# Attention of a hybrid decoder step: each head runs its four pairs of query blocks in a row, operands in pieces

## The chip, the cores and the metric

The kernel runs on one core of a Trainium2 chip. The metric is the device time of one execution in microseconds. The core has five engines, each with its own instruction queue: TensorE (PE; PEld are its weight loads), VectorE (DVE), ScalarE (ACT), GpSimd (POOL) and SyncE (SP), which issues the DMA transfers here. An engine works through its queue in order; between engines, semaphores make an instruction wait for its operands.

## What is computed

One layer of a hybrid decoder for a prompt of 1024 rows and 32 decode rows (8 sequences of 4). RMSNorm and one input projection feed a gated linear recurrence (4 heads) and a forgetting attention (8 heads of 64); both are gated, concatenated, projected back, added to x and normed. The change lies in the attention of the prompt, here for blocks of 128 queries (qb, cb: rows of q and c of the block; scale = D ** -0.5):

```python
def fox_prompt(q, k, v, log_f):
    c = jnp.cumsum(log_f, axis=1).transpose(0, 2, 1)
    ...
    def block(i):
        ...
        s = jnp.einsum('bqhd,bkhd->bhqk', qb, k).astype(jnp.float32) * scale
        s = s + (cb[..., None] - c[:, :, None, :])
        s = jnp.where(qpos[:, None] >= kpos[None, :], s, -jnp.inf)
        p = jax.nn.softmax(s, axis=-1)
        return jnp.einsum('bhqk,bkhd->bqhd', p.astype(v.dtype), v)
    o = lax.map(block, jnp.arange(nb))
    ...
```

## The kernel before

All matmuls keep fp32 accuracy by splitting operands into a high part (rounded to the fast fp32r format) and a low part (the rest), so a product of two operands takes three matmuls.

The order of all engines' work is written by hand (`manual_schedule`), by a Python program that mixes two strands. The first is the main loop: log-forget sums, the recurrence for four heads, then 32 attention steps. The second is the *stream*, a generator (`projections`) that yields a few matmuls at a time with an estimate of their time: the slabs of the input projection (128 columns each; `slab` L441 to 460, three chunks of 352 rows and 24 matmuls each, 0.45 us estimated for three), the values' transposes (`fox_values`), the gates (`fox_gate`), and later the output projection and the decode attention. `fill(us)` lets the stream go on for so many estimated microseconds. When the stream stands at a flag that the main loop has not raised (`wait_flag`), it yields nothing and the rest of that fill is lost. `need(mark)` runs the stream up to a mark. `defer(n, f)` records f after n more stream yields.

The attention works on four pairs of heads; a pair's q, k and v come from three slabs (buffers u0, u2, u5), its gate from a fourth. A *step* (`fox_step`) is one head and 256 queries, with q = 0 to 3 for the place of these queries in the prompt. It transposes the softmax rows of its two blocks (T, tile pt, L925), copies and subtracts them into a high and a low part (ACT L929, DVE L930), weighs the values with them (W, tile po), and meanwhile makes the scores (S, tile ps, three banks) of the next step's second block and the second-next step's first block: mask sum L894, reduction L895, exponential L905 with its row sum, reciprocal L908 on DVE, scaling L910 on POOL. `PLANS` gives the order within a step, with fractions at which the step's fill is spent. Work and widths grow with q.

Before the scores of a head can be made, `fox_prep` forms its operands: Q1 and K1 hold the high part of q or k in 64 partitions and the log-forget sums in the others (two small DMA loads from c_s), Q2 and K2 the high and low parts: two copies on ACT (L846, L852), two on DVE (L848, L851), one subtraction on POOL (L854) and one on DVE (L856), each over whole rows of 1024. The heads of a pair have separate buffers. The steps of a pair run in the order (head, q) = (0,0), (0,1), (1,0), (1,1), (0,2), (0,3), (1,2), (1,3), and both heads' preparation for the next pair stands in its last steps.

## Time and profile before

| | us |
|---|---|
| median of 3 timed runs | 782.65 (782.34 to 782.94) |
| profiled execution, its time | 779.85 |
| its span, first to last instruction | 778.1 |
| PE busy | 740.7 (95%) |
| DVE busy | 461.8 (59%) |
| ACT busy | 356.9 (46%) |
| POOL busy | 319.4 (41%) |

The span falls into the start and value projection (0 to some 90 us), gates and recurrence under which the slabs are made (to 350), the attention of the first three pairs under the remaining slabs (to 600), the last pair under output projection and decode attention (to 712), and the rest of the output projection. An engine's busy time in a stretch, set against the length of the stretch, tells how much of it the engine stood still; what ended a wait is given in brackets behind an instruction.

### The profile page before, as it was taken

Reading aid. Unit: us, or ns where it says so; the run is one execution under the profiler, and the core shown is the slowest. Engines: PE = TensorE matmul, PEld = TensorE weight load, DVE = VectorE, ACT = ScalarE, POOL = GpSimd, SP = SyncE. Lnnn points to the kernel's source line nnn. Section 1 sums busy time; section 2 is a strip of 40 time slices with the busy share of each in tenths; the row PEclk is TensorE's granted clock in tenths of the full one; section 3 lists DMA queues with packets and bytes.
Section 4 is the critical chain, followed back from the end, with each engine's and each line's share of the span. In section 5 each row is a group of like instructions: output and inputs, shape, how many; then the busy total and the mean of one; then the engine's idle time right before and its main releaser. Section 6 shows DMA issues by size and latency. Waiting matters only on the chain.

```text
span 778.1 us, 12930 instructions
## 1 busy us (share of the span) xinstructions
PE 740.7 (95%) x4815; PEld 659.7 (85%) x4815; DVE 461.8 (59%) x954; ACT 356.9 (46%) x833; POOL 319.4 (41%) x337
## 2 busy tenths in 40 slices
PE   6999899999999999998999989989999899999996
PEld 5678899998999999997998889979988676577886
DVE  7774324646647665267447844785478776667422
ACT  4562446444242441136546654757466522455312
POOL 4450435373471853535434462536344533332101
PEclk8999999999999999999999999999999999999999
DMA  8411000100221103003101020101111686713521
GB/s 300 134 34 34 1 29 3 60 26 36 84 80 59 55 31 109 29 32 123 44 28 57 29 82 28 57 29 55 55 56 57 210 304 221 258 56 130 190 81 55
DMA packets 28465, 64.99 MB, mean 84 GB/s; under 512 B 6290, under 2 KB 7442, under 8 KB 28402
## 3 DMA queue, kind: packets, MB, share of 16 engines
q1 hardware_dynamic: 28402, 64.16, 23.6%
q8 instruction: 38, 0.62, 0.3%
q14 instruction: 25, 0.20, 0.1%
HBM read 47.27 MB, written 16.88 MB: 82 GB/s over the span
## 4 chain that ended last, share of the span: by engine, by line
PE 71%; DVE 15%; ACT 7%; issue 4%; POOL 1%; DMA 1%; SPq 0%; DVEq 0%; ACTq 0%; POOLq 0%
PE pj L95 52%; PE ps L95 11%; PE po L95 3%; DVE u L856 2%; PE pt L925 2%; DVE u L930 2%; DVE st L895 2%; PE pt L95 1%; ACT u L905 1%; ACT u L929 1%; DMA u<-in_w_dram 1%; DVE u L812 1%; ACT xhi L269 1%; POOL u L311 1%; DVE u L791 1%
## 5 line engine op out<-in xcount | busy, mean ns | idle before, releaser
L95 PE MATMUL pj<-xhi,u 128*128 128x352 f32 x1152 | 315.2, 332 | 0.7 <-DVE u L449 0.5
L95 PEld LDWEIGHTS pj<-xhi,u 128*128 128x128 f32 x1152 | 205.8, 188 | 3.4 <-DVE u L449 0.8
L95 PE MATMUL pj<-xlo,u 128*128 128x352 f32 x576 | 186.2, 323 | 0.0
L95 PE MATMUL ps<-u,u 128*128 128x64 f32 (+7 forms) x952 | 129.7, 272 | 3.4 <-ACT u L905 2.6
L95 PEld LDWEIGHTS ps<-u,u 128*128 128x128 f32 (+2 forms) x952 | 111.8, 178 | 14.4 <-ACT u L905 4.4
L910 POOL TENSOR_SCALAR u<-u,st 128x128 f32<-128x128 f32 (+3 forms) x64 | 48.7, 761 | 153.8 <-DVE st L908 87.7
L95 PEld LDWEIGHTS pj<-xlo,u 128*128 128x128 f32 x576 | 108.6, 189 | 0.7
L95 PE MATMUL pj<-u,xhi 128*128 128x260 f32 (+1 forms) x384 | 90.3, 329 | 4.1 <-DVE u L488 2.2
L905 ACT ACTIVATE u<-ps,st 128x512 f32<-128x512 f32 (+2 forms) x96 | 55.0, 578 | 50.3 <-DVE st L898 21.6
L95 PE MATMUL pj<-h,u 128*128 128x512 f32 (+2 forms) x237 | 74.3, 384 | 0.8 <-DVE h L1046 0.8
L655 POOL TENSOR_TENSOR u<-u,u 128x256 f32<-128x256 f32 (+1 forms) x56 | 40.4, 721 | 84.4 <-PE ps L95 78.8
L95 PEld LDWEIGHTS pj<-u,xhi 128*128 128x128 f32 x384 | 63.9, 191 | 12.2 <-ACT xhi L269 2.5
L930 DVE TENSOR_TENSOR u<-pt,u 128x512 fp32r<-128x512 f32 (+1 forms) x80 | 48.5, 631 | 29.3 <-ACT u L929 28.7
L95 PE MATMUL pj<-u,xlo 128*128 128x260 f32 (+1 forms) x192 | 62.6, 326 | 2.9 <-DVE xlo L273 2.9
L95 PE MATMUL po<-u,u 128*128 128x256 f32 (+1 forms) x320 | 52.3, 287 | 9.3 <-DVE u L930 4.7
L929 ACT ACTIVATE u<-pt 128x512 fp32r<-128x512 f32 (+1 forms) x80 | 41.8, 552 | 41.9 <-PE pt L925 34.2
L895 DVE TENSOR_REDUCE st<-ps 128x1 f32<-128x512 f32 (+2 forms) x96 | 53.3, 556 | 12.4 <-PE ps L95 9.8
L95 PEld LDWEIGHTS po<-u,u 128*128 128x128 f32 x320 | 44.3, 188 | 16.7 <-DVE u L930 7.8
L95 PEld LDWEIGHTS pj<-h,u 128*128 128x128 f32 (+1 forms) x237 | 42.3, 185 | 10.7 <-ACT u L811 1.2
L95 PE MATMUL pj<-u,u 128*128 128x512 f32 (+3 forms) x174 | 46.8, 437 | 2.7 <-ACT u L1213 2.1
L95 PE MATMUL pj<-w,u 128*128 128x512 f32 (+2 forms) x125 | 47.8, 383 | 0.0
L656 POOL TENSOR_TENSOR u<-u,u 128x256 f32<-128x256 f32 (+1 forms) x56 | 43.7, 780 | 0.0
(242 smaller groups left out, 1144.0 us busy)
## 6 DMA issues: line engine op xcount, KB each, us to landing
u<-in_w_s_dram SPq DMA_DIRECT2D x24, 512.0 KB
out_dram<-u SPq DMA_DIRECT2D x12, 512.0 KB
u<-in_x_b_dram SPq DMA_DIRECT2D x8, 512.0 KB
u<-in_cache_k_t_dram SPq DMA_DIRECT2D x16, 256.0 KB
u<-in_cache_v_dram SPq DMA_DIRECT2D x16, 256.0 KB
m_s<-u SPq DMA_DIRECT2D x7, 512.0 KB
u<-m_s SPq DMA_DIRECT2D x14, 256.0 KB
w<-in_w_out_dram SPq DMA_DIRECT2D x12, 256.0 KB
```

The source lines that it names most:

```text
L95: PE.matmul(out, lhsT, rhs, start=start, stop=stop, skip_group_check=True)
L269: A.activation(xhi[:, k, t0:t0 + n], xt[:, k], AF.Copy)
L311: se[a].tensor_sub(l[:, a], raw[:, a], f32(h[:, a]))
L655: G.tensor_mul(k4[:, :, 0, :], k4[:, :, 0, :], f3[:, eb, 1:2].to_broadcast([128, n, m]))
L656: G.tensor_mul(q4[:, :, 1, :], q4[:, :, 1, :], f3[:, eb, 0:1].to_broadcast([128, n, m]))
L856: V.tensor_sub(K2[o], kf[r, :T], f32(K1[r]))
L895: V.tensor_reduce(st[:, m:m + 1], ps, axis=AX.X, op=OP.min)
L905: A.activation(P[:, s], ps, AF.Exp, scale=-1.0, bias=st[:, lo:lo + 1], accum_out=st[:, 2 + m:3 + m])
L910: G.tensor_scalar(P[:, :e], P[:, :e], st[:, 4:5], 1.0, op0=OP.mult, op1=OP.mult)
L925: PE.transpose(p[:, c:c + 128], probs[n, b][:, j * 128:(j + 1) * 128], ident)
L929: A.activation(ph[:, :w], p[:, :w], AF.Copy)
L930: V.tensor_sub(pl[:, :w], p[:, :w], f32(ph[:, :w]))
```

## The change

Four things change. The order of the steps: each head now runs q = 0, 1, 2, 3 in a row. The fills: a table per pair and step in place of four numbers by q and a factor for the last pair. The operands: they are made in pieces of a chunk (352 or 320 columns) or half a row (512); for head 0 of the later pairs the pieces are deferred from the eviction of each chunk of the q and k slabs, for head 1 they run as eight pieces over the last step of a pair and the first steps of the next; the query's subtraction is on DVE, not on POOL. The stream's wait ahead of the next pair's slabs: it was the flag that both heads are prepared, now a flag `free` raised after the second step of the pair, since head 1's preparation still reads u0 and u2 until then.

```diff
         i = slabs.index(C_FQ + pr * 128)
         qf, kf, vf = U(0), U(2), U(5)
-        yield from slab(i, f"fq{pr}", lambda ps, a, b: A.activation(qf[:, a:b], ps, AF.Copy, scale=-FD ** -0.5))
+
+        def evac(dst, which, scale):
+            def f(ps, a, b):
+                A.activation(dst[:, a:b], ps, AF.Copy, scale=scale)
+                if pr:
+                    defer(2, operand_hi, pr, 0, which, slice(a, min(b, T)))
+                    defer(5, operand_lo, pr, 0, which, slice(a, min(b, T)))
+            return f
+
+        if pr:
+            sums_in(pr, 0)
+        yield from slab(i, f"fq{pr}", evac(qf, 0, -FD ** -0.5))
         V.tensor_copy(qd[:, pr], qf[:, T:])
-        yield from slab(i + 1, f"fk{pr}", lambda ps, a, b: A.activation(kf[:, a:b], ps, AF.Copy))
+        yield from slab(i + 1, f"fk{pr}", evac(kf, 1, 1.0))
...
+    def operand_hi(pr, i, which, t):
+        r, o = slice(64 * i, 64 * i + 64), slice(64 - 64 * i, 128 - 64 * i)
+        x, X1, X2 = U((0, 2)[which]), QS(i)[which], QS(i)[2 + which]
+        V.tensor_copy(X1[r, t], x[r, t])
+        A.activation(X2[r if which else o, t], x[r, t], AF.Copy)
+
+    def operand_lo(pr, i, which, t):
...
+        V.tensor_sub(X2[o if which else r, t], x[r, t], f32(X1[r, t]))
+        if which and t.stop == T:
+            flags.add(f"prep{pr}{i}")
+
     def fox_prep(pr, i):
 
-        h, qf, kf = 2 * pr + i, U(0), U(2)
...
-        A.activation(Q2[o], qf[r, :T], AF.Copy)
-        SP.dma_start(f32(Q1[b0:b0 + 2]), cr)
-        V.tensor_copy(Q1[r], qf[r, :T])
-        SP.dma_start(f32(K1[b0 + 2:b0 + 4]), cr)
-        V.tensor_copy(K1[r], kf[r, :T])
-        A.activation(K2[r], kf[r, :T], AF.Copy)
-        G.tensor_sub(Q2[r], qf[r, :T], f32(Q1[r]))
-        V.tensor_sub(K2[o], kf[r, :T], f32(K1[r]))
+        sums_in(pr, i)
+        for c in range(2):
+            for which in range(2):
+                operand_hi(pr, i, which, slice(512 * c, 512 * c + 512))
+                yield
+                operand_lo(pr, i, which, slice(512 * c, 512 * c + 512))
+                yield
...
-    order = [(pr, i, q) for pr in range(4) for i, q in ((0, 0), (0, 1), (1, 0), (1, 1), (0, 2), (0, 3), (1, 2), (1, 3))]
+    order = [(pr, i, q) for pr in range(4) for i in range(2) for q in range(4)]
...
-        po, tt = po_[0], tt2[:, i]
+        po, tt = po_[0], tt2[:, n // 2 % 2]
...
-                yield from wait_flag(f"prep{pr}1")
+                yield from wait_flag(f"free{pr}")
...
     for i in range(2):
-        preps.append(fox_prep(0, i))
+        fox_const(i)
+    preps.append(fox_prep(0, 0))
+    for _ in range(8):
         fill(0.6)
-        fox_const(i)
-        for _ in range(4):
-            prep_step()
-            fill(0.77)
+        prep_step()
+    preps.append(fox_prep(0, 1))
...
+    FILL = ((4.8, 6.8, 6.2, 5.4) * 2,) * 3 + ((4.8, 6.8, 8.5, 8.0, 11.0, 10.5, 8.5, 7.0),)
     for n, (pr, i, q) in enumerate(order):
         s = n % 8
+        fox_step(n, FILL[pr][s])
         if pr == 3 and s == 0:
+            prep_step(True)
             flags.add("values")
             for k in range(4):
                 m_load(k, 0)
             for k in range(2):
-                defer(8 + 4 * k, m_split, k, 0)
-        fox_step(n, (7.6, 6.4, 4.4, 3.0)[q] * (F3 if pr == 3 else 1))
-        prep_step(True)
-        if s == 4 and pr < 3:
+                defer(7 + 3 * k, m_split, k, 0)
+        if s == 1:
+            prep_step(True)
+            flags.add(f"free{pr}")
+        if s == 6 and pr < 3:
             need(f"fk{pr + 1}")
-            preps.append(fox_prep(pr + 1, 0))
-        if s == 6 and pr < 3:
             preps.append(fox_prep(pr + 1, 1))
+        if s == 7 and pr < 3:
             need(f"v{pr + 1}")
```

In the changed program most lines stand further down: the copies of operands are L861 and L862, their subtraction L867, the values' eviction, cast and subtraction L796, L802 and L803, the mask sum, reduction and exponential L915, L916 and L926, the turned rows' copy and subtraction L950 and L951.

PE in pair 0, second step: the end of its weighing (po) and the scores (ps) that follow. Before, with the stream's slab (pj) around them:

```order
L95 MATMUL po_105<-u_3375,u_3252 128x128
L95 MATMUL pj_184<-xhi,u_732 128x352
L95 MATMUL pj_184<-xlo,u_732 128x352
L95 MATMUL pj_184<-xhi,u_733 128x352
...
L95 MATMUL ps_147<-u_3273,u_3272 128x384
L95 MATMUL ps_147<-u_3284,u_3283 128x384
L95 MATMUL pj_183<-xhi,u_732 128x352
```

Now, up to the third step's scores:

```order
L95 MATMUL po_105<-u_3350,u_3256 128x128
L95 MATMUL ps_146<-u_3234,u_3233 128x512
...
L95 MATMUL ps_147<-u_3242,u_3241 128x384
L946 MATMUL pt_1143<-cc,u_95 128x128
...
L946 MATMUL pt_1144<-cc,u_96 128x128
L95 MATMUL ps_145<-u_3234,u_3233 128x512
...
L95 MATMUL ps_146<-u_3242,u_3241 128x512
L95 MATMUL pj_183<-xhi,u_732 128x352
```

Before, 18 matmuls of the stream stand between weighing and scores and 18 behind them; now weighing, scores, the third step's transposes (pt) and its scores follow each other with none between.

DVE in the last steps of pair 0. Before, around the key's subtraction L856 (st are the row statistics):

```order
L895 TENSOR_REDUCE st_1105<-ps_147 128x1
L898 TENSOR_REDUCE st_1105<-st_1105 128x1
L856 TENSOR_TENSOR u_3238<-u_1118,u_3234 64x1024
L957 TENSOR_TENSOR u_101<-u_101,po_105 64x512
L907 TENSOR_REDUCE st_1105<-st_1105 128x1
L908 RECIPROCAL st_1105<-st_1105 128x1
L930 TENSOR_TENSOR u_3375<-pt_1143,u_3374 128x512
```

Now, in the last step, with pieces for head 1 of the next pair:

```order
L916 TENSOR_REDUCE st_1102<-ps_145 128x1
L861 CAST u_3237<-u_1117 64x512
L867 TENSOR_TENSOR u_3383<-u_1117,u_3237 64x512
L951 TENSOR_TENSOR u_3350<-pt_1144,u_3349 128x512
L951 TENSOR_TENSOR u_3350<-pt_1143,u_3349 128x384
L929 RECIPROCAL st_1102<-st_1102 128x1
L861 CAST u_3238<-u_1118 64x512
L915 TENSOR_TENSOR ps_146<-ps_146,cc 128x128
L916 TENSOR_REDUCE st_1103<-ps_146 128x1
L867 TENSOR_TENSOR u_3384<-u_1118,u_3238 64x512
L802 CAST u_4055<-u_100 128x4x64
```

The one subtraction over 1024 columns has become pieces of 512 between the steps' own instructions, and the values' casts follow them.

ACT at the first values (u_100 takes them from the transposes pt). Before:

```order
L774 ACTIVATE u_1115<-pj_183 128x352
L846 ACTIVATE u_3237<-u_1117 64x1024
L852 ACTIVATE u_3238<-u_1118 64x1024
L785 ACTIVATE u_100<-pt_1143 128x512
L785 ACTIVATE u_100<-pt_1144 128x512
```

Now:

```order
L785 ACTIVATE u_1115<-pj_183 128x352
L862 ACTIVATE u_3241<-u_1117 64x512
L862 ACTIVATE u_3242<-u_1118 64x512
L796 ACTIVATE u_100<-pt_1143 128x512
L862 ACTIVATE u_3241<-u_1117 64x512
L796 ACTIVATE u_100<-pt_1144 128x512
```

Two half rows instead of two whole rows stand ahead of the first of the values' evictions.

## Rows read from the trace of the kernel before

**Rows 1.** The page: span, and each engine's busy time, share, instructions.

```profile
span 778.1 us, 12930 instructions
PE 740.7 (95%) x4815; PEld 659.7 (85%) x4815; DVE 461.8 (59%) x954; ACT 356.9 (46%) x833; POOL 319.4 (41%) x337
```

**Rows 2.** By stretch: length; busy time (instructions) by engine; granted clock, DMA share, GB/s.

```profile
340.00:376.00 36.00, 33.04 (x206) 31.14 (x205) 26.42 (x51) 21.10 (x49) 16.33 (x16) 1.00 0.25 90
376.00:420.00 44.00, 43.99 (x293) 42.93 (x292) 20.90 (x57) 23.20 (x55) 17.38 (x17) 1.00 0.14 48
420.00:452.00 32.00, 26.99 (x175) 24.22 (x174) 27.62 (x52) 20.08 (x48) 17.40 (x15) 1.00 0.10 36
452.00:496.00 44.00, 44.00 (x292) 43.26 (x290) 19.80 (x56) 23.36 (x61) 18.00 (x20) 1.00 0.10 38
496.00:532.00 36.00, 31.65 (x208) 28.77 (x207) 30.99 (x61) 24.30 (x53) 17.19 (x16) 1.00 0.13 47
576.00:600.00 24.00, 21.25 (x144) 19.16 (x143) 20.91 (x46) 16.62 (x36) 10.06 (x10) 1.00 0.20 68
612.00:624.00 12.00, 8.56 (x29) 5.68 (x29) 7.16 (x11) 3.76 (x8) 5.29 (x6) 0.86 0.84 300
```

**Rows 3.** Order of time, first values: start, length, engine, line [idle before, releaser].

```profile
354.11 1.05 ACT L846 ACTIVATE u<-u 64x1024 fp32r<-64x1024 f32 x1
355.18 1.06 ACT L852 ACTIVATE u<-u 64x1024 fp32r<-64x1024 f32 x1
356.76 0.28 PE L795 MATMUL pt<-cc,u 128*32 128x128 f32 x1 [2.08 <-ACT u L785]
356.81 0.41 PE L95 MATMUL pj<-xhi,u 128*128 128x352 f32 x1
...
360.77 0.34 PE L95 MATMUL ps<-u,u 128*128 128x128 f32 x2
```

**Rows 4.** Order of time, from the first mask sum to the first weighing.

```profile
362.10 0.30 DVE L894 TENSOR_TENSOR ps<-ps,cc 128x128 f32<-128x128 f32 x1
...
365.68 0.82 POOL L910 TENSOR_SCALAR u<-u,st 128x128 f32<-128x128 f32 x2
...
368.91 0.48 ACT L929 ACTIVATE u<-pt 128x384 fp32r<-128x384 f32 x1
...
370.03 0.56 PE L95 MATMUL po<-u,u 128*128 128x256 f32 x3 [0.20 <-DVE u L930]
```

**Rows 5.** One line's instructions: count, ns min/median/max, first and last start.

```profile
L856 DVE TENSOR_TENSOR u<-u,u x8: 1221/3084/3391, 351.8 to 601.1; 64x1024 fp32r<-64x1024 f32 x8
L854 POOL TENSOR_TENSOR u<-u,u x8: 2383/2396/3252, 351.4 to 601.0; 64x1024 fp32r<-64x1024 f32 x8
```

**Rows 6.** Order of time, boundary from pair 0 to pair 1.

```profile
422.55 1.03 PE L95 MATMUL po<-u,u 128*128 128x256 f32 x8
...
424.36 3.22 DVE L856 TENSOR_TENSOR u<-u,u 64x1024 fp32r<-64x1024 f32 x1
...
428.54 1.27 DVE L930 TENSOR_TENSOR u<-pt,u 128x512 fp32r<-128x512 f32 x2
...
429.27 1.22 PE L95 MATMUL po<-u,u 128*128 128x256 f32 x7 [0.47 <-DVE u L930]
```

**Rows 7.** Groups on DVE, 340 to 620 us: count, busy us, mean ns, idle before.

```profile
L895 DVE TENSOR_REDUCE st<-ps 128x1 f32<-128x512 f32 x37 | 25.4, 687 | 9.2 <-PE ps L95 8.4
L930 DVE TENSOR_TENSOR u<-pt,u 128x512 fp32r<-128x512 f32 x36 | 23.6, 684 | 14.3 <-ACT u L929 14.0
```

**Rows 8.** Stretches of 2 us at the turn to the output projection, columns as rows 2.

```profile
614.00:616.00 2.00, 0.11 (x1) 0.00 (x0) 0.83 (x3) 1.21 (x3) 1.07 (x2) 1.00 0.86 245
618.00:620.00 2.00, 1.36 (x4) 0.93 (x5) 1.62 (x3) 0.44 (x2) 0.20 (x1) 0.73 1.04 394
620.00:622.00 2.00, 2.00 (x7) 1.61 (x6) 0.00 (x0) 0.18 (x1) 0.94 (x1) 0.50 1.05 410
622.00:624.00 2.00, 2.00 (x10) 1.65 (x9) 1.04 (x3) 0.00 (x0) 0.00 (x0) 0.92 1.04 386
```

17 lines of the change are left out of this document (8 added, 9 removed).

## Prediction

> **What bounds the kernel now.** The page first [rows 1]: TensorE (PE) is busy 740.7 of 778.1 us, 95%, and no other engine passes 59%. All work of PE stays in the changed program, so a change of order can only move PE's 37.4 us of idle time. I therefore read the busy times by stretch next [rows 2]. In each row the reader takes the stretch's length minus PE's busy time. From 376 to 420 and from 452 to 496 us PE has no gap, and VectorE (DVE) is busy 47% and 45% of the time. The gaps lie where DVE is busy 86% or more: 5.0 us in 420 to 452, 4.35 in 496 to 532, 2.75 in 576 to 600. These are the boundaries between one pair of heads and the next: 12.1 us together. Two other places matter: the opening of the attention, 340 to 376, with 2.96 us idle, and the turn to the output projection, 612 to 624, with 3.44 us. The rest is the kernel's start, the recurrence and the last 18 us, which the change does not touch.
>
> Why the boundaries stall is in the order of time [rows 6]: L856, one subtraction over 1024 columns, holds DVE for 3.22 us; the sum L930 that the weighing matmuls need stands behind it and starts at 428.54, and PE waits. Of L856's eight instances the shortest took 1.22 us and the median was 3.08 [rows 5]; GpSimd's twin L854 (median 2.40 us) runs at the same time.
>
> **The change part by part.** The sum is made on the profiled execution, 779.85 us with a span of 778.1; it lies 2.8 us under the median of 782.65, and I add the difference that I find to the median.
>
> *First values.* PE's first gap is 2.08 us long and ends with the copies L785 [rows 3]. Ahead of these on ScalarE (ACT) stand two copies of whole rows, each 1.05 us. Now two copies of half rows stand there, 0.53 us each by half the width. L785 comes 1.05 us sooner, and the gap shrinks to about 1.0.
>
> *The opening's filler.* This is the largest term. PE has no gap as long as matmuls of the stream (the projections' slabs) stand between steps of the attention. Before, the stream may go on to the next pair's slabs once both heads' operands are made, ahead of the first step. Now it waits for a flag raised after the second step. Until then only the gate's slab is left, 72 matmuls. By the order, from the values' transposes to the first scores of the third step there stood 144 stream matmuls and now stand those 72. 24 of them took 3.96 us [rows 3], 0.165 each, so 11.9 us of cover leave this stretch. What is left for PE there: 72 x 0.165 = 11.9 us, plus 18 transposes and 12 weighings at 0.13 (eight took 1.03 [rows 6]) = 3.9 us, plus scores of 9216 columns, at 0.165 us per 352 columns 4.3 us: 20.1 us in all.
>
> Now the chain of the other engines. Two sections have to be waited out. (a) From the first mask sum to the second weighing, 362.10 to 370.03, took 7.9 us [rows 4]. It now begins when DVE has made the casts and subtractions of the values and the second half of the first head's operands, which I estimate at 360.0 from the start of L785 and the durations of rows 5 and 7. With the same length the weighing comes at about 368. PE's own work from 356 to there is 39 stream matmuls (6.4 us) and 1.7 us of attention, so it is at 364: 4 us idle (2.5 to 5). (b) From the second step's seven transposes to the third step's weighing hardly any stream is left (12 matmuls). DVE alone has some 11.5 us of instructions there, an estimate from their count: 0.69 for a reduction or a sum of 512 columns [rows 7], three pieces of the other head's operands, the gate's sums. In between lie waits in a ring: scores wait for a bank that the exponential of the last scores frees, the exponential for the reduction, the transposes for both. I go through the ring by the durations in rows 4 and 7 and reach 14 us where PE has 8.2 us of work: 6 us idle (3 to 8). With the gap of 1.0 at the values the opening idles 11 us instead of 2.96: **a loss of 8** (3.5 to 11). I choose near the middle, since rows 4 are the same chain with the same instructions in it.
>
> *The boundaries.* Per pair the steps now run 0, 1, 2, 3, 0, 1, 2, 3 and each has its own fill (4.8, 6.8, 6.2, 5.4 us instead of 7.6, 6.4, 4.4, 3.0). The old fifth and sixth steps, which had two of the widest score blocks each and the small fills 4.4 and 3.0, are gone. Head 0's operands are made chunk by chunk as the slabs arrive, the blocks of 3 us fall into pieces of 512 or 352 columns, and L854 leaves GpSimd. What remains: head 1's eight pieces still fall into the last step and the next pair's first, together with the values. I add DVE's instructions of these two steps: 16.4 us, against 17 us of PE work. The old stretch of 496 to 532 had 31.0 us of DVE and idled 4.35 in 36 [rows 2], 12%; at that rate 17 us idle 2; I take 1.7 at each of three boundaries, 5 us (2 to 7.5). Besides, in pairs 1 and 2 the stream has run to the flag at the end of the second step: 3 matmuls stand where 18 were planned. That leaves 2.5 us of cover out, twice; part of it is waited for: 2.4 us together (0 to 4). Of 12.1 us remain 7.4: **a gain of 4.7** (0.6 to 10).
>
> *What costs nothing.* The copies of operands stay as many columns; 14 more instructions on DVE and 6 on ACT in each later pair come from the cutting and lie beside PE outside the boundaries. The two small loads of sums for each head are issued on SP ahead of a slab and wait for the last scores of the former head; behind them stand only weights that are needed a slab later. If that cover fails, a slab's weights are late; the nearest row is the turn, where PE idled 3.44 us over late operands [rows 2].
>
> *The last pair.* Its fills shrink from 77 us to 65, so 12 us of output projection move behind the attention, where PE runs without gaps anyway: nothing. The loads of the merged rows start a step later, and the wait of 3.44 us at the turn stays: **+0.3** (-1 to +2).
>
> Sum: +8 - 4.7 + 0.3 = +3.6 us, from 782.65 to about 786.
>
> **The rivals.** *The boundaries win.* If steps of even weight remove the DVE blocks nearly whole (2 us left, a gain of 10) and the ring in the opening runs at DVE's pace (a loss of 3.5), the time is 776. For it speaks that PE has no gap wherever DVE is under half busy, and over a whole pair it is 64%. Against it stand the values and eight pieces still in the same two steps. It decides at an opening loss equal to the boundaries' gain. *The two cancel:* 781.1 to 784.2. *The clock.* At 614 to 616 us PE was busy 0.11 of 2 us; from 618 on the granted clock was 0.73, 0.50, 0.92 in three rows of 2 us [rows 8], 0.50 being 1.2 instead of 2.4 GHz. That gives away 0.54 + 1.0 + 0.16 = 1.7 us. The gap of 2.08 us in the opening left the clock at 1.00 [rows 2, 3]. If the thin stretch of the opening brings it down, the time is 788. *Subtractions that block each other.* The query half's subtraction moves from GpSimd to DVE. If the halves cost what full rows did at L856's median, 1.54 us each instead of 0.61, a head needs 3.7 us more of DVE, and the boundaries gain about 2 instead of 4.7: 789. For it speaks that GpSimd is still busy half of the boundary (17.4 of 32 us [rows 2]); against it, that L854 was the partner of most of the long ones.
>
> The Trainium skill, page "SBUF — State Buffer", section "Who interferes with whom", has a rule on this last case: a VectorE instruction with two inputs in SBUF contends with a GpSimd instruction that reads SBUF, and the one that starts first keeps the other out until it ends. The trace agrees as far as 1.22 against 3.08 us goes. By that rule the change is good for the key half, which loses its partner, and bad for the query half, which GpSimd made without delaying anything but L856.
>
> **How the numbers follow.** The forecast of 786 has 0.33, the clock 0.15, the blocked subtractions 0.10: slower 0.58. The cancelling case has 0.20, the boundaries' win 0.22. A difference of 0.2%, 1.6 us, is about what a measurement of this kernel can tell from none, and the chances go by that bound. The range reaches from 778.5, which takes in half of the winning case, to 791.5, which holds the opening's loss at its upper end with the gain of the sum, and most of the clock's case.
>
> **What would show it.** Right: the gap that L785 ended falls from 2.08 to about 1 us; in the first 40 us of the attention PE idles 8 to 13 us, with waits of score matmuls for the exponentials and of weighings for copies and sums of the transposed rows; at the boundaries 1 to 2 us each; no DVE instruction of 3 us left there. Wrong: the opening idles under 6 us (the ring is faster than I added up), or the three boundaries together idle under 3 us, or pair 3 and the projection behind it show gaps that were not there.

## The result, and the profile after

The changed kernel takes 802.5 us (median of 4 runs, 799.14 to 803.98) where the kernel before, run beside it, takes 782.8: a ratio of 1.0239 (1.0215 to 1.0264). The forecast was 786.0 with a range up to 791.5. The sign was right; the size was not.

The page of the profiled execution, 803.72 us, against [rows 1]:

```profile
span 801.9 us, 12979 instructions
PE 754.6 (94%) x4815; PEld 668.3 (83%) x4815; DVE 475.7 (59%) x1006; ACT 360.4 (45%) x855; POOL 304.1 (38%) x329
```

The same 4815 matmuls. PE's idle time grew by 9.9 us (37.4 to 47.3), but its busy time grew too, by 13.9. Where, the stretches say (length; busy time and instructions of PE, PEld, DVE, ACT, POOL; granted clock, DMA share, GB/s), against [rows 2]:

```profile
340.00:360.00 20.00, 18.76 (x126) 17.93 (x126) 14.78 (x31) 8.97 (x22) 4.05 (x4) 1.00 0.34 124
360.00:380.00 20.00, 15.60 (x87) 14.42 (x86) 10.76 (x30) 9.75 (x27) 6.64 (x9) 0.91 0.13 42
380.00:400.00 20.00, 14.28 (x74) 12.13 (x74) 14.91 (x32) 12.23 (x29) 3.80 (x4) 0.83 0.00 1
400.00:440.00 40.00, 38.58 (x255) 37.19 (x254) 27.05 (x63) 21.17 (x54) 16.38 (x17) 1.00 0.08 27
440.00:480.00 40.00, 37.78 (x249) 35.56 (x248) 27.50 (x65) 27.07 (x66) 16.92 (x18) 1.00 0.22 68
...
600.00:620.00 20.00, 19.08 (x131) 18.12 (x130) 14.90 (x33) 12.11 (x27) 8.33 (x10) 1.00 0.39 125
620.00:640.00 20.00, 14.67 (x72) 12.12 (x71) 14.50 (x32) 11.59 (x29) 9.05 (x8) 0.86 0.49 166
640.00:660.00 20.00, 18.39 (x96) 15.59 (x95) 13.07 (x28) 7.46 (x21) 7.56 (x7) 0.93 0.76 272
```

Length minus PE's busy time is idle; busy time times one minus the granted clock is what the halved clock gave away. The opening, 340 to 400, idles 1.24 + 4.40 + 5.72 = 11.4 us (3.0 before) and loses 1.4 + 2.4 = 3.8 to the clock (nothing before). From 400 to 620 it idles 9.6 us; the three stretches of 40 us left out repeat those above them to 0.02 us. The boundaries before had 12.1. The turn, 620 to 660, idles 6.9 us (3.4 before) and loses 2.1 + 1.3 = 3.4 to the clock (1.7 before).

The opening in order of time (start, length, engine, line; in brackets PE's idle time just before and who ended it), against [rows 3, 4]:

```profile
358.13 0.28 PE L806 MATMUL pt<-cc,u 128*32 128x128 f32 x1 [1.23 <-ACT u L796]
...
362.94 0.28 DVE L915 TENSOR_TENSOR ps<-ps,cc 128x128 f32<-128x128 f32 x1
...
366.32 0.44 PE L946 MATMUL pt<-cc,u 128*128 128x128 f32 x2 [1.22 <-POOL u L931]
...
370.45 0.38 PE L95 MATMUL po<-u,u 128*128 128x256 f32 x1 [2.26 <-ACT u L950]
371.54 0.73 PE L95 MATMUL po<-u,u 128*128 128x256 f32 x3 [0.71 <-DVE u L951]
...
386.67 1.01 PE L95 MATMUL ps<-u,u 128*128 128x384 f32 x2 [3.22 <-ACT u L926]
389.01 1.76 PE L946 MATMUL pt<-cc,u 128*128 128x128 f32 x7 [1.12 <-POOL u L931]
```

These are the waits that the prediction named: the values 1.23 us (2.08 before), the weighing for the turned copy (L950 is the old L929), a score for the exponential that frees its bank (L926). From the first mask sum to the second weighing it takes 8.6 us, 7.9 before. What it had left out of the sum stands in the stretches of 2 us, same columns, against [rows 8]:

```profile
384.00:386.00 2.00, 0.00 (x0) 0.00 (x0) 1.61 (x5) 0.16 (x1) 0.00 (x0) 0.85 0.00 0
386.00:388.00 2.00, 1.22 (x3) 0.71 (x3) 0.83 (x3) 1.67 (x5) 0.34 (x1) 0.50 0.00 0
388.00:390.00 2.00, 0.99 (x5) 1.00 (x6) 1.87 (x6) 0.00 (x0) 0.95 (x1) 0.50 0.00 0
390.00:392.00 2.00, 2.00 (x8) 1.71 (x7) 0.98 (x5) 1.87 (x5) 0.00 (x0) 0.50 0.00 0
```

PE stood still for 2 us, and the granted clock is at 0.50 (1.2 GHz) for the next six. At the turn the second half of the merged rows' splitting is late on ACT and then on GpSimd:

```profile
633.68 0.50 PE L95 MATMUL pj<-u,u 128*128 128x512 f32 x1 [2.05 <-ACT u L1234]
...
636.07 2.50 PE L95 MATMUL pj<-u,u 128*128 128x512 f32 x5 [1.89 <-POOL u L1235]
```

Last, how long the last pair and what follows it (the tail) take. The line's 20 subtractions of turned rows (L930 before, L951 after) in the last pair, with the first and the last start; before, then after:

```profile
L930 DVE TENSOR_TENSOR u<-pt,u x20: 535/687/692, 606.4 to 710.0; 128x512 fp32r<-128x512 f32 x12, 128x384 fp32r<-128x384 f32 x8
```

```profile
L951 DVE TENSOR_TENSOR u<-pt,u x20: 547/684/692, 616.5 to 718.5; 128x512 fp32r<-128x512 f32 x12, 128x384 fp32r<-128x384 f32 x8
```

The pair takes 103.6 us before and 102.0 after; from there to the end of the span it is 68.1 before and 83.4 after. Twelve us of output projection were moved behind the attention. The tail grew by 15.3, and the pair shrank by 1.6 only: of the 23.8 us between the two spans, 10.1 have come about when the last pair starts and 13.7 come behind that.

### The profile page after: what moved, and what is told of

The parts are those of the page before. It is cut to its first block, busy times and chain, and to the rows that moved or that the text cites. A ratio compares the mean times of both kernels' runs of the same rounds, so it can differ in the third digit from the quotient of the medians.

```text
span 801.9 us, 12979 instructions
## 1 busy us (share of the span) xinstructions
PE 754.6 (94%) x4815; PEld 668.3 (83%) x4815; DVE 475.7 (59%) x1006; ACT 360.4 (45%) x855; POOL 304.1 (38%) x329
## 4 chain that ended last, share of the span: by engine, by line
PE 68%; DVE 14%; ACT 9%; issue 4%; POOL 2%; DMA 1%; SPq 0%; DVEq 0%; ACTq 0%; POOLq 0%
PE pj L95 48%; PE ps L95 10%; PE po L95 5%; ACT u L926 3%; PE pt L946 3%; DVE st L916 2%; DVE u L951 1%; PE pt L95 1%; DVE u L867 1%; DVE u L861 1%; DMA u<-in_w_dram 1%; DVE ps L915 1%; ACT xhi L269 1%; POOL u L311 1%; ACT u L950 1%
## 5 line engine op out<-in xcount | busy, mean ns | idle before, releaser
L931 POOL TENSOR_SCALAR u<-u,st 128x128 f32<-128x128 f32 (+3 forms) x64 | 53.6, 837 | 175.8 <-DVE st L929 155.1
L926 ACT ACTIVATE u<-ps,st 128x512 f32<-128x512 f32 (+2 forms) x96 | 55.0, 577 | 64.3 <-DVE st L919 32.5
L655 POOL TENSOR_TENSOR u<-u,u 128x256 f32<-128x256 f32 (+1 forms) x56 | 40.4, 721 | 84.4 <-PE ps L95 78.8
L95 PE MATMUL po<-u,u 128*128 128x256 f32 (+1 forms) x320 | 54.2, 292 | 15.5 <-DVE u L951 9.3
L950 ACT ACTIVATE u<-pt 128x512 fp32r<-128x512 f32 (+1 forms) x80 | 42.2, 553 | 50.4 <-PE pt L946 47.9
L951 DVE TENSOR_TENSOR u<-pt,u 128x512 fp32r<-128x512 f32 (+1 forms) x80 | 48.9, 634 | 26.1 <-ACT u L950 25.2
L916 DVE TENSOR_REDUCE st<-ps 128x1 f32<-128x512 f32 (+2 forms) x96 | 53.4, 557 | 12.7 <-PE ps L95 10.5
L95 PE MATMUL pj<-u,u 128*128 128x512 f32 (+3 forms) x174 | 50.4, 442 | 4.7 <-ACT u L1234 2.0
L946 PE MATMUL pt<-cc,u 128*128 128x128 f32 x288 | 44.5, 284 | 2.5 <-POOL u L931 2.5
```

The lines of the kernel that those rows point to most:

```text
L95: PE.matmul(out, lhsT, rhs, start=start, stop=stop, skip_group_check=True)
L655: G.tensor_mul(k4[:, :, 0, :], k4[:, :, 0, :], f3[:, eb, 1:2].to_broadcast([128, n, m]))
L916: V.tensor_reduce(st[:, m:m + 1], ps, axis=AX.X, op=OP.min)
L926: A.activation(P[:, s], ps, AF.Exp, scale=-1.0, bias=st[:, lo:lo + 1], accum_out=st[:, 2 + m:3 + m])
L931: G.tensor_scalar(P[:, :e], P[:, :e], st[:, 4:5], 1.0, op0=OP.mult, op1=OP.mult)
L946: PE.transpose(p[:, c:c + 128], probs[n, b][:, j * 128:(j + 1) * 128], ident)
```

## The experiments

All runs are set against runs of the kernel before on the same chip; the ratio is to those. The runs stand on several chips, so two of them are best set against each other by their ratios; where the medians tell another difference, both are given. One more number is worked out from the program and not from a trace: how much planned fill finds the stream at a flag and is lost, in the planner's own microseconds. It is 0 in the kernel before; in the changed one 5.5 in the first pair's second step and 2.1 in that of the second and the third pair, 9.7 in all.

### The opening: the late flag, the cover, the clock

**The late flag alone, in the old order.**

```diff
-                yield from wait_flag(f"prep{pr}1")
+                yield from wait_flag(f"free{pr}")
...
+        if s == 1:
+            flags.add(f"free{pr}")
```

> The kernel before, with one edit of the change alone: the stream waits for a flag raised after each pair's second step instead of the flag that both heads are prepared. Theory A (the late flag takes the filler out of the opening, whatever the order of the steps): the opening starves as in the changed kernel, the time is 10 to 14 us above the kernel before, 793 to 797. Theory B (the starving comes of the order of the steps or of the pieces): the time is that of the kernel before or up to 3 us above it, 783 to 786.

817.34 us, 1.0440 (1.0404 to 1.0476): 34 us, three times theory A. The planner loses 16.9 us of fill here: 10.5 in the first pair and 3.2 in each of the next two. The flag costs far more without the new order than with it.

**Dummies in place of the lost fill**, where the stream stands at its flag in the first two steps.

```diff
             if c is None:
+                if spare[0]:
+                    p = ps_pj()[:, :352]
+                    for _ in range(int(debt[0] / 0.16)):
+                        mm(p, xhi[:, 0, :128], xhi[:, 0, :352], True, True)
                 debt[0] = 0.0
...
+        spare[0] = pr == 0 and s < 2
```

> The changed kernel, with dummy matmuls of 352 columns (results unused) put into the first pair's first two steps wherever the stream stands at its flag and a fill is lost; 34 or so in all, 5.6 us of TensorE work. Theory A (the opening's thin stretch costs by the clock as well as by the chain): the granted clock from 360 to 400 us is 1.00, the dummies lie in time that TensorE idles, and the run is 3 to 5 us faster than the changed kernel, about 798. Theory B (only the chain of the other engines sets the opening, the clock there costs nothing): the run is the same as the changed kernel, 802 to 803. Theory C (TensorE is the bound even there): slower by the dummies' 5.6 us, about 808.

803.44 us, 1.0251 (1.0229 to 1.0272): theory B. Idle time from 380 to 400 us fell from 5.7 to 2.3 and the time did not move. Cover that does nothing useful only stands where PE stood still.

**The flag raised at once in the first pair**, both heads' operands made ahead of it. The second pair's first head then gets its operands in the fourth to sixth step, and the first pair's fills (the same sum) stand earlier.

```diff
-    preps.append(fox_prep(0, 0))
...
-    preps.append(fox_prep(0, 1))
+    for i in range(2):
+        preps.append(fox_prep(0, i))
+        for _ in range(8):
+            fill(0.46)
+            prep_step()
+        prep_step(True)
+    flags.add("free0")
...
+        if n == 3:
+            need("fk1")
+            preps.append(fox_prep(1, 0))
```

> The changed kernel, with the opening of the first pair as before the change in one respect: both heads' operands (in pieces) are made ahead of the first step and the flag is raised there, so that the stream never stands at it; the second pair's first head then gets its operands as eight pieces in the fourth to sixth step instead of with the slabs, and the first pair's fills are shifted forward by 3.4 us in sum. Theory A (the late flag's missing filler is what the opening loses): TensorE's idle and half-clock time from 345 to 400 us falls from 18 to 5 us or so and the run takes 788 to 793. Theory B (the opening starves of VectorE's and ACT's chain whatever stands between): above 798. Theory C (eight pieces more ahead of the first step only move the loss there): 795 to 800.

802.14 us, 1.0266 (1.0202 to 1.0329): the opening was cured for the most part (5.2 us idle from 340 to 400 instead of 11.4), the time was not, so none of the three as written. Its stretches, columns as above:

```profile
360.00:380.00 20.00, 16.78 (x96) 15.92 (x95) 14.50 (x33) 12.83 (x31) 6.81 (x9) 0.91 0.13 41
380.00:400.00 20.00, 20.00 (x133) 19.61 (x132) 9.91 (x29) 10.48 (x29) 7.54 (x8) 1.00 0.09 27
...
440.00:460.00 20.00, 17.47 (x118) 16.60 (x116) 15.21 (x33) 15.70 (x36) 9.12 (x10) 1.00 0.09 27
460.00:480.00 20.00, 17.53 (x84) 14.96 (x85) 11.29 (x32) 11.51 (x30) 4.94 (x6) 0.74 0.00 1
```

From 380 to 400 us PE has no gap left. From 440 to 480 it idles 5.0 us and the clock gives away another 4.6, where the changed kernel idled 2.2 at full clock. The planner says why: the work that the stream did sooner is missing ahead of the next pair's flag, and 10.2 us of fill are lost in the second pair's first two steps. The starving had moved by one pair.

**The cover spread**: the same, with the first pair's fills cut from 46.4 to 36.2 us, and the last pair with its values and fills as before the change (below).

```diff
-    FILL = ((6.8, 6.8, 6.8, 6.2, 4.8, 5.8, 4.6, 4.6),) + ((4.8, 6.8, 6.2, 5.4) * 2,) * 2 + ((4.8, 6.8, 8.5, 8.0, 11.0, 10.5, 8.5, 7.0),)
+    FILL = ((5.2, 5.2, 4.8, 4.2, 4.2, 4.6, 4.0, 4.0),) + ((4.8, 6.8, 6.2, 5.4) * 2,) * 2 + ((13.7, 11.5, 7.9, 5.4) * 2,)
```

> The changed kernel with the first pair opened as in the run with the flag raised at once, the first pair's fills cut from 46.4 to 36.2 us and evened so that the stream no longer runs dry in the second pair's first steps, and the last pair's values, loads and fills as before the change. Theory A (the late flag takes about ten us of the stream's work out of the cover once, and that loss is small when it is spread over a pair): the opening gains 8 us on the changed kernel, the first boundary loses 2 instead of 11, the last pair gains 7: 786 to 790. Theory B (the loss of cover costs the same wherever it stands): 794 to 797.

789.97 us, 1.0093 (1.0059 to 1.0127): theory A by the time. Against the run with the old last pair and the opening of the changed kernel (1.0189, below) this takes off 7.5 us by the ratios, 5.7 by the medians. The stretches from 340 us to the last pair's first turned rows, in that run and in this one:

```profile
340.00:400.00 60.00, 49.43 (x280) 45.66 (x279) 40.22 (x91) 30.78 (x76) 14.30 (x16) 0.89 0.16 56
400.00:616.60 216.60, 208.81 (x1375) 199.85 (x1374) 149.13 (x349) 129.10 (x314) 91.12 (x91) 1.00 0.16 51
```

```profile
340.00:400.00 60.00, 54.73 (x345) 52.09 (x344) 41.31 (x98) 33.03 (x83) 19.53 (x21) 0.97 0.18 63
400.00:611.00 211.00, 198.80 (x1296) 188.18 (x1295) 141.71 (x337) 125.59 (x304) 85.56 (x85) 1.00 0.15 49
```

The idle time is hardly less: 10.6 + 7.8 = 18.4 us there, 5.3 + 12.2 = 17.5 here. So theory A's reason, that the loss is small when it is spread, does not show; what PE no longer idles in the opening it idles later. What has gone is most of the halved clock, 5.4 us given away there and 1.6 here. The late flag's price is a matter of place in this sense only: in one lump the missing cover brings the clock down too.

**Dummies ahead of the waiting matmuls**, 86 in all, in the opening and at the turn, so that the clock is not halved there; `spin(k)` is k matmuls into a bank that nobody reads.

```diff
+        if n in (0, 2) and j2 == 0:
+            spin(6)
         p = ps_t()
...
+            if tb == c == 0 and k == 1:
+                spin(11, woh(0, cs))
             mm(ps, h[:, t], woh(k, cs), k == 0, False)
```

> The changed kernel, with dummy matmuls (results unused) directly ahead of the matmuls that waited longest: at the values 6, in the first pair's steps 18 ahead of a score and 6 to 12 ahead of transposes and weighings, 21 wide ones ahead of the second set of operands of the output projection, 7 ahead of a weighing of the last pair; each group fills about the wait that stood there and should delay nothing. Theory A (the half clock in the opening and at the turn, 8 us of the difference between the two kernels, is set off by those waits and costs what it shows): the granted clock is 1.00 from 340 to 720 us and the time falls by 5 to 8 us to 795 to 797. Theory B (while the clock is halved TensorE waits for others anyway): the clock is restored and the time stays within 2 us of 802.5.

802.11 us, 1.0249 (1.0203 to 1.0295). The clock came back whole at the turn and from 380 to 400 us (from 360 to 380 it stayed at 0.91):

```profile
380.00:400.00 20.00, 17.63 (x107) 15.26 (x106) 15.03 (x32) 12.14 (x30) 4.18 (x4) 1.00 0.01 2
620.00:640.00 20.00, 17.07 (x101) 15.34 (x100) 15.44 (x34) 12.13 (x31) 10.09 (x9) 1.00 0.45 152
640.00:660.00 20.00, 18.93 (x103) 15.67 (x102) 14.19 (x29) 6.89 (x20) 7.29 (x7) 1.00 0.82 283
```

The time did not move, which is theory B, but the run is no clean proof: dummies waited themselves for a bank of PSUM, once 3.0 us in the opening and once 1.5 at the turn. Another price of the clock comes from the kernel before, whose granted clock differs from run to run: at 0.992 it took 779.85 to 780.49 us, at 0.983 it took 783.6 to 786.0, about 0.5 us for each 0.001. The changed kernel's four runs stand at 0.977 to 0.987, around 0.980, and the middle of the others at 0.986: some 3 us of the 19.7, if the clock is the cause of that spread and not its companion. In this run, at 0.989 to 0.993, no time came back. What the halved clock costs is not settled.

### The last pair

**The values ahead of the last pair's first step**, as before the change.

```diff
-        fox_step(n, FILL[pr][s])
         if pr == 3 and s == 0:
...
-                defer(7 + 3 * k, m_split, k, 0)
+                defer(8 + 4 * k, m_split, k, 0)
+        fox_step(n, FILL[pr][s])
```

> The changed kernel, with the flag for the last pair's values, the four loads of merged rows and the distance of their splitting as before the change, that is ahead of the last pair's first step and not behind it. Theory A (the merged rows loaded a step later cost the turn to the projection): TensorE's idle time from 620 to 664 us falls from 7.0 to about 4.5 us, one of the two halvings of the clock goes, and the run is 4 to 6 us faster than the changed kernel, 797 to 799. Theory B (the turn's gaps come of the order of ACT's and VectorE's work in the last pair's first two steps): no change, 802 to 803.

803.56 us, 1.0254 (1.0237 to 1.0271): theory B.

**The same, with the last pair's old fills.**

```diff
-    FILL = ((4.8, 6.8, 6.2, 5.4) * 2,) * 3 + ((4.8, 6.8, 8.5, 8.0, 11.0, 10.5, 8.5, 7.0),)
+    FILL = ((4.8, 6.8, 6.2, 5.4) * 2,) * 3 + ((13.7, 11.5, 7.9, 5.4) * 2,)
```

> The changed kernel, with the last pair's values, loads and fills as before the change (13.7, 11.5, 7.9, 5.4 for each head, 77 us in all, and the values ahead of its first step); only the order of the steps differs there. Theory A (thin fills in the last pair's first steps cause its loss of 10 us): TensorE's idle and half-clock time behind 620 us falls by 6 to 10 us, the run takes 793 to 797. Theory B (the heavy steps that now meet the turn to the output projection cause it): 800 to 804.

795.65 us, 1.0189 (1.0144 to 1.0234): theory A, below the run without these fills by 5.1 us by the ratios and 7.9 by the medians.

**The thin fills in the old order**: the kernel before with `F3 = 1.52` in place of 1.8, 65 us in the last pair instead of 77.

> The kernel before, with the factor of the last pair's fills cut from 1.8 to 1.52, so that they are 65 us in all as in the changed kernel and not 77; everything else as before. Theory A (12 us of the output projection moved behind the attention leave TensorE without cover in the last pair's steps): 4 to 8 us above the kernel before, 787 to 790. Theory B (the prediction's: they move to where TensorE runs without gaps and cost nothing): within 1 us of the kernel before.

790.36 us, 1.0094 (1.0067 to 1.0121): 7.4 us, theory A, and the plainest refutation of the prediction's "nothing". Its last pair and its span:

```profile
core 0 of [0], span 786.5 us
...
L930 DVE TENSOR_TENSOR u<-pt,u x20: 545/680/692, 607.6 to 705.3; 128x512 fp32r<-128x512 f32 x12, 128x384 fp32r<-128x384 f32 x8
```

The pair is 5.9 us shorter, the tail 13.1 longer. Idle time does not show it: it rose by 0.7 us in the whole span, while PE's busy time rose by 7.7 with the same 4815 matmuls. Over half of that lies in 32 of them, with which the decode attention weighs its values; the stream makes them in the last pair's fills. From 600 us on, before and in this run (count, time in which at least one of them is busy, mean ns of one):

```profile
L95 PE MATMUL pj<-u,u 128*32 128x512 f32 x32 | 9.1, 602 | 0.0
```

```profile
L95 PE MATMUL pj<-u,u 128*32 128x512 f32 x32 | 13.2, 603 | 0.7 <-DVE u L1132 0.7
```

One of them takes as long as ever. But in a row they overlap, and two by themselves take more than half of what fourteen take. In order of time, the first of them before, then two groups of this run:

```profile
666.89 1.93 PE L95 MATMUL pj<-u,u 128*32 128x512 f32 x14
```

```profile
688.27 1.05 PE L95 MATMUL pj<-u,u 128*32 128x512 f32 x2
689.84 1.04 PE L95 MATMUL pj<-u,u 128*32 128x512 f32 x2
```

The thinner fills hand them out in smaller groups: eight of the eleven here are of two, four of the seven before.

**More than the old fills**: `F3 = 2.1`, 90 us.

> The kernel before, with the factor of the last pair's fills raised from 1.8 to 2.1 (90 us in all); everything else as before. Theory A (more cover in the last pair helps still): 1 to 4 us below the kernel before. Theory B (the last pair has no idle time left to cover, and more output projection ahead only comes earlier): within 1 us of the kernel before.

792.36 us, 1.0113 (1.0087 to 1.0139), against both theories: too much is as bad as too little. By the starts of the turned rows the pair takes 117.6 us here and the tail 63.0, so it grows by 14.0 where the tail shrinks by 5.1.

**The new order in the last pair alone**, everything else as before.

```diff
-    order = [(pr, i, q) for pr in range(4) for i, q in ((0, 0), (0, 1), (1, 0), (1, 1), (0, 2), (0, 3), (1, 2), (1, 3))]
+    order = [(pr, i, q) for pr in range(3) for i, q in ((0, 0), (0, 1), (1, 0), (1, 1), (0, 2), (0, 3), (1, 2), (1, 3))]
+    order += [(3, i, q) for i in range(2) for q in range(4)]
```

> The kernel before, with the new order of steps (each head's four in a row) in the last pair alone; fills by q as before (77 us in all), operands, flag and the other pairs as before. By the planner's count 4.5 us of fill find the stream at a flag in the sixth and seventh step, since the rows that the next part of the output projection needs are gated two steps later. Theory A (the order itself costs in the last pair): 4 to 8 us above the kernel before, with the longer tail behind the attention. Theory B (the order costs nothing by itself): within 1.5 us.

788.83 us, 1.0068 (1.0044 to 1.0092): theory A, at 5.3 us.

```profile
core 0 of [0], span 785.3 us
...
L931 DVE TENSOR_TENSOR u<-pt,u x20: 546/679/692, 607.8 to 711.2; 128x512 fp32r<-128x512 f32 x12, 128x384 fp32r<-128x384 f32 x8
```

The pair takes 103.4 us as before, and the tail 74.1 instead of 68.1: the stream stood at a flag for 4.5 us of its fill, since the first half of the merged rows is complete when both heads have run q = 1, and the second head now does so two steps later. The thin fills of the changed kernel lose nothing at that flag. They are still the worse choice there: with the old fills it is faster, though 3.0 us of them are lost.

### The operands in pieces

**Pieces in all pairs, old order, query subtraction on VectorE.** The kernel before with the changed `sums_in`, `operand_hi`, `operand_lo` and `fox_prep`, and in the opening

```diff
-        for _ in range(4):
+        for _ in range(8):
             prep_step()
-            fill(0.77)
+            fill(0.385)
+        prep_step(True)
```

> The kernel before, with the operands in pieces alone: eight pieces of half rows for each head, the query's subtraction on VectorE, the order of the steps, the fills and the flag as before. Theory A (the blocks of 3 us on VectorE make the boundaries stall): the idle time of the three boundaries falls from 12.1 to 8 or 9 us and the time by 3 to 4, to about 779. Theory B (the sum of VectorE's work there makes them stall, and it grows by the query's subtraction): the time is the same or 1 to 2 us above, 783 to 785.

793.25 us, 1.0114 (1.0091 to 1.0137): worse than both theories; part of it lay in the opening, which this run had not meant to change. So it was made again **with the first pair left alone** (`if pr == 0` with the old instructions in `fox_prep`):

> The kernel before, with the operands in eight pieces of half rows for the later three pairs alone; the first pair's are made as before. Order, fills and flag as before. Theory A (what the pieces cost in the run of pieces alone, 9.6 us, is the opening's): 783 to 786, with the three boundaries' idle time at 12 to 14 us. Theory B (the pieces cost at the boundaries and the turn): 789 to 793.

789.78 us, 1.0104 (1.0061 to 1.0146): theory B, 8 us. Then **with the query's subtraction back on GpSimd**:

```diff
-        V.tensor_sub(X2[o if which else r, t], x[r, t], f32(X1[r, t]))
+        (V if which else G).tensor_sub(X2[o if which else r, t], x[r, t], f32(X1[r, t]))
```

> The kernel before with the operands in pieces for the later three pairs, as in the run of that name, but with the query's subtraction left on GpSimd. Theory A (VectorE's added work at the boundaries is what the pieces cost): 2.8 us per head come off VectorE, the time falls by 5 to 8 from 789.8 to that of the kernel before or a little below it. Theory B (the cutting costs it: more instructions, each with its semaphores, and what is left of the pieces in a row at a step's end): within 2 us of 789.8. Theory C (GpSimd's and VectorE's subtractions keep each other out, and GpSimd's delays the scaling of the softmax rows): above 792.

779.96 us, 0.9955 (0.9935 to 0.9975): theory A, and 3.5 us faster than the kernel before. The pieces gain; the exchange of engines costs 11.7 us by the ratios, 9.8 by the medians, in this order. These subtractions on VectorE from 410 to 620 us (count, busy us, mean ns, idle before), in the run without GpSimd and in the run with it:

```profile
L856 DVE TENSOR_TENSOR u<-u,u 64x512 fp32r<-64x512 f32 x24 | 19.3, 806 | 0.7
```

```profile
L856 DVE TENSOR_TENSOR u<-u,u 64x512 fp32r<-64x512 f32 x12 | 11.7, 974 | 0.4
```

And PE's costliest wait in the same stretch (us in total, times, longest), in the same order:

```profile
PE po L95 <- DVE u L958: 10.0, 9, 2.2
```

```profile
PE po L95 <- DVE u L958: 6.3, 8, 1.5
```

VectorE makes half as many with GpSimd's help, is held 7.6 us less, and the weighings wait 3.7 us less for its sums. The means do not tell what GpSimd's subtractions do to VectorE's: the twelve that stay are the key's, which took 0.93 us in the other run, too, against 0.97 here. The clock has a part in the difference: from 400 to 620 us its halving gave away 6.2 us in the run without GpSimd and 3.0 in the run with it.

**The same exchange in the changed kernel, and in the run with the cover spread.**

> The changed kernel, with the query's subtraction of all pieces on GpSimd as before the change, not on VectorE. Theory A (the exchange costs in the changed kernel what it cost in the old order, 10 us): 792 to 795. Theory B (with the pieces of the first head spread along the slabs VectorE has room, and the exchange is free, as in the run with the spread cover): 801 to 803.

> The run of the changed kernel with the cover spread and the last pair as before, with the query's subtraction of all pieces on GpSimd as before the change. Theory A (VectorE's added work is the 7 us that remain): 783 to 786. Theory B (the cutting or the order is): 788 to 792.

798.95 us, 1.0188 (1.0159 to 1.0217), between the two theories, 4 us below the changed kernel; and 789.06 us, 1.0084 (1.0058 to 1.0110), theory B, the same as the run without the exchange back. In these two the exchange costs less than in the old order. That VectorE has room where the first head's pieces lie spread was the reason expected, and no run takes it apart.

Here the two engines' effect on each other shows. The half rows subtracted on VectorE from 410 to 620 us, in the changed kernel and with the query's on GpSimd (columns as above):

```profile
L867 DVE TENSOR_TENSOR u<-u,u 64x512 fp32r<-64x512 f32 x12 | 8.3, 688 | 0.4
```

```profile
L867 DVE TENSOR_TENSOR u<-u,u 64x512 fp32r<-64x512 f32 x6 | 6.7, 1116 | 0.2
```

With GpSimd's subtractions about, one half takes 1.12 us in the mean instead of 0.69. The two do slow each other, as the Trainium skill, page "SBUF — State Buffer", section "Who interferes with whom", has it of a VectorE instruction with two inputs in SBUF and a GpSimd instruction that reads SBUF; the trace agrees. But VectorE then makes half as many and is held 1.6 us less by them: the contention is the smaller price.


### What beats both

**The old order with the first three pairs' fills evened.**

```diff
-        fox_step(n, (7.6, 6.4, 4.4, 3.0)[q] * (F3 if pr == 3 else 1))
+        fox_step(n, (6.2, 5.2, 5.8, 5.2, 5.6, 5.2, 5.0, 4.6)[s] if pr < 3 else (7.6, 6.4, 4.4, 3.0)[q] * F3)
```

> The kernel before, with the fills of the first three pairs evened over the eight steps (6.2, 5.2, 5.8, 5.2, 5.6, 5.2, 5.0, 4.6 instead of 7.6, 6.4, 7.6, 6.4, 4.4, 3.0, 4.4, 3.0; the same sum); the order, the operands and the flag as before. Theory A (small fills beside the heaviest steps make the boundaries stall, as the prediction had it): the three boundaries idle 8 to 9 us instead of 12.1 and the time falls by 2 to 4, to 779. Theory B (the boundaries stall on VectorE's work there whatever the fills): within 1 us of the kernel before; more if the openings of the pairs, which lose cover, stall.

780.13 us (10 runs), 0.9960 (0.9946 to 0.9974): theory A, 3.1 us faster than the kernel before. A part of this gain, and of that of the pieces above, goes with the clock. At a granted clock of 0.988 alone, the kernel before took 781.78 to 782.48 us, this run 779.72 to 781.87 and the run of the pieces with GpSimd 780.37 to 782.05: about 2 us remain.

**Evened in the last pair too** (12.6, 10.6, 12.0, 10.2, 8.6, 7.4, 8.6, 7.0 there), and **evened with the pieces** of the later pairs, the query's subtraction on GpSimd:

> The kernel before with the fills evened in all four pairs: the first three as in the run of evened fills, the last 12.6, 10.6, 12.0, 10.2, 8.6, 7.4, 8.6, 7.0 instead of 13.7, 11.5, 13.7, 11.5, 7.9, 5.4, 7.9, 5.4 (the same sum of 77 us). Theory A (evening helps wherever heavy steps had the small fills): 1 to 3 us below the run of evened fills, 777 to 779. Theory B (the last pair idles 0.4 us behind its turn and has nothing to give): the same as that run, 780.

> The kernel before with the two parts that gained: the operands of the later three pairs in pieces, the query's subtraction left on GpSimd, and the fills of the first three pairs evened. Order and flag as before. Theory A (both take away different idle time at the boundaries): 776 to 778, 5 to 7 us below the kernel before. Theory B (both take away the same idle time): 779.5 to 780.5.

789.54 us, 1.0097 (1.0064 to 1.0129), against both theories: in the last pair evened fills cost. The pair and its tail take 10.0 us longer than before the change, and the 32 matmuls of the decode attention 13.9 us of PE instead of 9.1. And 785.26 us (12 runs), 1.0014 (0.9994 to 1.0034), against both: the two gains do not add. Two of the twelve runs took 780.8 and 780.9 at a granted clock of 0.991, the other ten 784.8 to 787.3 at 0.984 or 0.985.

## Why the prediction was wrong

*First values.* Right: the gap fell from 2.08 to 1.23 us; 1.0 was forecast.

*The opening.* The chain of the other engines was followed rightly: 11 us idle were forecast and 11.4 came, in the waits that were named, and no instruction that had been thought hidden stood in the path. The term of 8 was too small by the clock. A halving that cost 3.8 us by the record stood as a rival of its own with 0.15 and 1.7 us, though the prediction itself had put 72 matmuls where 144 had been and knew from [rows 8] that the clock falls behind a thin stretch. By the record it belonged in the sum, and with it the opening costs 12 us of PE's time; the dummies, which undid a part of it, won no time, so the 3.8 are an account and not a measured price. The sentence on the cover, "11.9 us of cover leave this stretch", was the right one; what it lacked is that they leave it for good: the run with the flag raised at once shows much of the loss one pair later, and the run with the cover spread idles nearly as much in all as the one that it is built on.

*The boundaries.* The sign was right, the size half: of 12.1 us remain 9.6, a gain of 2.5 where 4.7 was forecast, inside the bounds of 0.6 to 10. The rule "at that rate 17 us idle 2" held: the stretches with a boundary idle 2.2. What was left out are the 1.4 us in each of the other stretches, which had no gap before. The cause was mixed up as well. Evening the fills gains 3.1 us by itself and the pieces 3.5, but the pieces' gain is taken back by the exchange of engines that came with them: 4 us in the changed kernel, 10 to 12 in the old order. The rival of the blocked subtractions had this exchange and its price of 3 us with the chance 0.10, for another reason: halves of L867 that take 1.54 us each. At the boundaries they take 0.69 (the changed kernel's line under "The operands in pieces"). It is not that they are slow, but that VectorE makes them at all.

*The last pair.* This is the step that failed: "+0.3 (-1 to +2)", with the sentence "12 us of output projection move behind the attention, where PE runs without gaps anyway: nothing". In its place the two profiled executions show 13.7 us. Two parts of it show in runs of their own. In the old order the thin fills alone cost 7.4 us, and putting the old fills back in the changed kernel gives 5.1 to 7.9. And with the old fills the new order of the steps costs 5.3 by itself, since it makes the merged rows late. PE did run without gaps behind the attention, so the argument looked only at where the work went. It did not ask what the work had done where it came from: taken out of the last pair, 12 us shorten it by 5.9. Nor did it see that the fills' size sets how the moved work itself runs. From 600 us on, the 32 matmuls of the decode attention take 9.1 us before, and in the changed kernel and then with the old fills:

```profile
L95 PE MATMUL pj<-u,u 128*32 128x512 f32 x32 | 12.2, 602 | 0.7 <-DVE u L1153 0.7
```

```profile
L95 PE MATMUL pj<-u,u 128*32 128x512 f32 x32 | 7.9, 600 | 0.0
```

So the premise at the head of the prediction, "a change of order can only move PE's 37.4 us of idle time", failed as well: of the 23.8 us between the spans 9.9 are idle time and 13.9 are busy time of PE for the same matmuls, the halved clock's part among them. The bounds were drawn around the wait at the turn, the one gap that the rows showed, and neither the new gaps nor a longer busy time were in them. "Pair 3 and the projection behind it show gaps that were not there" had been written down as what would make the prediction wrong, and it did.

*The sum.* Between the two profiled executions: opening +12.2 in place of +8 (idle 8.4, clock 3.8), boundaries -2.5 in place of -4.7, together 9.7 where the last pair starts 10.1 us later; the last pair and the tail +13.7 in place of +0.3. That is 23.4 of 23.8 us. The medians lie 19.7 apart, because the profiled execution of the kernel before is 3.0 us under its median and that of the changed kernel 1.2 above its own. By the runs, the last pair's part is 10 to 13 us.

*What stays open.* The thin fills in the old order raise PE's busy time by 7.7 us. 4.1 of these are the decode attention's matmuls, and 1.4 are halved clock, ahead of 340 us where the two programs are alike; what the rest is, the rows do not tell. Nor was it tried to keep these matmuls in a row with the thin fills, which would show how much time the 4.1 are worth. It is open what the halved clock costs, and why the gains of the pieces and of the evened fills do not add; ten of that run's twelve executions show a lower clock than the other two and are 4 us slower, so the clock may have a part in it, but which gap sets it off was not tried.

## What to carry to other kernels

Where one stream of matmuls fills the gaps of another, its work is a stock that is used up: a flag that opens later takes away as much cover as the stream would have done in that time, and curing one place moves the hole to the next. Cost work that is moved at both ends, at the place it leaves as much as at the place it goes to; a place without gaps can be without gaps because of that work. Look at PE's busy time as well as at its gaps: 32 matmuls that were handed out in smaller groups kept PE busy a third longer here. And take a change of several parts apart: here two of its parts (evened fills; pieces without the exchange of engines) each make the kernel 3 us faster, and the rest of it cost some 20.

## What the runs showed of the hardware

The granted clock fell to 0.50 behind shorter waits than the prediction had allowed for. The gap of 2.08 us in the opening before the change had left it at 1.00 [rows 2, 3]; in the last pair after it, 1.27 us with 0.34 more right behind were followed by 0.62 and 0.53:

```profile
657.22 0.38 PE L95 MATMUL po<-u,u 128*128 128x256 f32 x1 [1.27 <-ACT u L950]
657.95 0.62 PE L95 MATMUL po<-u,u 128*128 128x256 f32 x3 [0.34 <-DVE u L951]
```

```profile
658.00:660.00 2.00, 2.00 (x11) 2.00 (x12) 1.12 (x3) 0.57 (x1) 0.00 (x0) 0.62 0.66 214
660.00:662.00 2.00, 2.00 (x9) 1.60 (x8) 0.69 (x1) 0.03 (x1) 0.00 (x0) 0.53 0.17 61
```

One gap's length did not tell whether the clock would fall. And the record is no price: across the runs of the kernel before, 0.001 of granted clock, 0.78 us of the span by the record, went with about 0.5 us, and the run with dummies, some 0.010 above the changed kernel, was no faster.

Matmuls with 32 columns of weights and 512 of data (128*32, 128x512 in the rows), 0.60 us each by the record, overlapped: fourteen in a row took 1.93 us, and two by themselves 1.05. So the cost of such a matmul depends on what stands beside it in the queue.
